# Modulation blocks 8 to 19 move from the head groups to the input projection, and small matmuls of the head groups alternate array halves

## The chip, the cores and the metric

The kernel runs on one core of a Trainium2 chip. The metric is the device time of one execution in microseconds (us), as the median of the runs. [...]

## The reference

One layer of a hybrid decoder, for a prompt of 512 tokens and for eight sample tokens. D is 2048, there are 16 attention and 16 RWKV-7 heads of 64.

```python
mod = jnp.dot(jax.nn.silu(c), P['ada_w'][l]) + P['ada_b'][l]     # (9, 2048) x (2048, 12288)
sh1, sc1, gt1, sh2, sc2, gt2 = jnp.split(mod, 6, axis=-1)
h = modulate(rmsnorm(x, P['norm1_g'][l]), sh1, sc1)
qa, ka, va, rkv0 = jnp.split(h @ w_in, [D_ATT, 2 * D_ATT, 3 * D_ATT], axis=-1)
...                                                              # attention heads -> att
wkv, y = wkv_scan(...)                                           # RWKV-7 heads -> rw
mix = jnp.concatenate([att, rw], axis=-1) @ P['w_out'][l]
x = x + gt1[:, None, :] * mix
h2 = modulate(rmsnorm(x, P['norm2_g'][l]), sh2, sc2)
gate, up = jnp.split(h2 @ P['w_gu'][l], 2, axis=-1)
x = x + gt2[:, None, :] * ((jax.nn.silu(gate) * up) @ P['w_down'][l])
```

The modulation has nine conditioning rows (one prompt, eight samples). Its 12288 columns are worked in 24 blocks of 512: blocks 0 to 7 are sh1 and sc1, which the input projection needs; 8 to 11 are gt1, 12 to 15 sh2, 16 to 19 sc2 and 20 to 23 gt2, which are first needed after the head groups.

## The kernel before

The program is one list of instructions for five engines. A scheduler sets each engine's order when the kernel is built, from its own timeline, so an engine takes its instructions strictly in that order on the chip, DMA issues included: nearly all loads and stores are issued by SP, in one queue.

It has these stages. **Start** (0 to about 200 us): normalise, transpose, modulation blocks 0 to 7. **LoRA** sums. **Input projection** (lines 783 to 802): 24 products, first the twelve of the RWKV columns (names p00 to p32), then the twelve of the attention columns (q00 to q32). Each product (line 133) covers 256 output columns by a Strassen scheme with seven PSUM banks, over eight pairs of k tiles, 21 matmuls a pair; weight columns come through two buffers (`raw`, two pairs each), are combined by VectorE (L143 to L146), split into a high and a low part by ScalarE and VectorE (L149, L150), and the seven sums are combined on VectorE (L163 to L170, tile c_p or c_q). After each pair of k tiles product calls `hook`, here `side` (line 783), which takes one step of the urgent generators (what follows on the last product: `rwkv_in`, `attn_in`) and, at every second call, one step of the lazy ones (`rwkv_pre`, bias table). All this side work shares one PSUM bank, the tag `ps`.

**Head groups** (lines 805 to 1297): for each of eight head pairs `rwkv_pair` (r), `chain` (c) and `attn_pair` (a), in the order of the string `SEQ_` at line 1282; `f3` there takes three steps of `todo`. `todo` holds modulation blocks 8 to 23 (line 865): `ada_steps` (line 231) loads four k tiles of 512 columns at a time (1 MB, tile raw_ada, two buffers), multiplies each k tile on its own column group of 32 (c_st holds the nine rows padded to 32), adds over k in PSUM (tile ada), copies the sum to SBUF and sums the four column groups by four matmuls with `sel4`. `rwkv_pair` makes, per pair: pg (the Gram products), a 16x16 inverse on VectorE that goes through DRAM both ways, then pq, px, pxt (64x64 each), pq and px of 32x32, pat, pgv, pu and pxa; `chain` walks the eight chunks (pch) and makes zy and z2; `attn_pair` makes pz (scores), pzt (transposes) and po (values), and the sample tokens' attention over the cache (K, V).

Where a loop runs over c or h outside and over the blocks i or b inside, all matmuls on one half of the array's rows (or columns) stand before those on the other half:

```python
for c in range(2):
    for i in range(8):
        mm(px[hb[c], i, :], Q[hb[c], i, :], XX[0][hb[c], i, :])
        mm(pxt[hb[c], i, :], XX[0][hb[c], i, :], Q[hb[c], i, :])
```

`hb` are the partitions 0 to 63 and 64 to 127. The output projection and the feed-forward part follow (from about 1505 us on).

## Time and profile before

| | us |
|---|---|
| median of three runs | 3356.26 (3343.64 to 3372.01) |
| the profiled execution | 3378.55 |
| its span, first to last instruction | 3376.8 |
| its mean granted clock | 0.918 |

| engine | busy us | share of the span |
|---|---|---|
| PE (matmul) | 2981.6 | 88% |
| DVE (VectorE) | 2480.9 | 73% |
| ACT (ScalarE) | 1278.0 | 38% |
| POOL (GpSimd) | 212.9 | 6% |

Busy time is the union of an engine's instructions; PEld is TensorE's weight load, which overlaps PE. Matmuls are pipelined, so a matmul's duration is longer than its distance to the next one. A group of rows gives the line of the kernel that issued it; line 90 is the helper `mm`, which all matmuls share, so groups are told apart by their tiles. An arrow in a row names what ended an engine's wait. The DMA share is the mean busy share of the core's 16 DMA engines.

### The profile page before, as it was taken

The page shows a single profiled execution, that of the slowest core. Times are in us where ns is not written, and L with a number is a line of the kernel's source. Part 1 is how long each engine was busy: PE and PEld are TensorE (multiplying, and loading weights), DVE is VectorE, ACT ScalarE, POOL GpSimd, SP SyncE. Part 2 cuts the span into 40 slices and gives each one's busy share as a digit, 9 for nine tenths or more (in the row PEclk, how much of TensorE's full clock was granted, in tenths as well). Part 3 has the DMA queues.
Part 4 walks back from the last instruction along what each step waited for, and adds up shares of the span by engine and source line. Part 5 has one row for each costly group of instructions (what it writes and reads, how often), then busy time and mean ns, then how long its engine had stood idle before and what let it go on. Part 6 is the DMA issues. An engine that isn't in the chain of part 4 may idle for free.

```text
span 3376.8 us, 59004 instructions
## 1 busy us (share of the span) xinstructions
PE 2981.6 (88%) x23282; PEld 2629.4 (78%) x23282; DVE 2480.9 (73%) x4846; ACT 1278.0 (38%) x2041; POOL 212.9 (6%) x216
## 2 busy tenths in 40 slices
PE   6987888999889999977977999999999987888988
PEld 2477787889746666656967999999999987787878
DVE  5666788777557455656878787778777788889786
ACT  3353343334223343444434333333333343334333
POOL 0100122110012111101000000000000000000000
PEclk8978999999858798887988999999999998999999
DMA  7744444444579798933322333333333332323223
GB/s 255 232 139 154 147 159 157 133 146 140 175 223 282 201 239 232 249 103 117 109 78 69 113 104 104 108 112 107 113 101 113 109 125 96 99 94 119 85 94 104
DMA packets 449194, 476.17 MB, mean 141 GB/s; under 512 B 84110, under 2 KB 360547, under 8 KB 448916
## 3 DMA queue, kind: packets, MB, share of 16 engines
q1 hardware_dynamic: 438736, 452.16, 43.4%
q10 hardware_dynamic: 7428, 11.65, 1.0%
q0 software_dynamic: 2752, 8.60, 0.8%
q8 instruction: 182, 2.98, 0.4%
q14 instruction: 96, 0.79, 0.1%
HBM read 409.10 MB, written 68.17 MB: 141 GB/s over the span
## 4 chain that ended last, share of the span: by engine, by line
PE 35%; DVE 28%; DMA 23%; issue 5%; ACT 5%; SPq 1%; POOL 1%; ACTq 0%; DVEq 0%; POOLq 0%
PE ada L90 4%; DMA raw_ada<-in_ada_w 2%; SPq L130 1%; PE po L90 1%; DVE x_a L125 1%; PE lx L90 1%; PE pg L90 1%; PE pz L90 1%; PE px L90 1%; DMA K<-in_cache_k 1%; PE pch L90 1%; PE pq L90 1%; DMA xb<-in_ada_w 1%; PE q22M L90 1%; PE q31M L90 1%
## 5 line engine op out<-in xcount | busy, mean ns | idle before, releaser
L90 PE MATMUL ada<-raw_ada,c_st 128*32 128x512 f32 x584 | 123.7, 763 | 17.5 <-DMA raw_ada<-in_ada_w 16.8
L90 PE MATMUL ada<-xb,c_st 128*32 128x512 f32 x184 | 69.9, 673 | 15.9 <-DMA xb<-in_ada_w 13.8
L1037 ACT ACTIVATE Sall<-pch,ppl 64x64 f32<-64x64 f32 x128 | 39.5, 309 | 75.5 <-PE pch L90 57.7
L1238 POOL TENSOR_TENSOR K<-K,qb 128x1024 f32<-128x1024 f32 (+2 forms) x24 | 58.2, 2440 | 147.5 <-DMA K<-in_cache_k 91.6
L1188 ACT ACTIVATE z<-z,mx 128x128 f32<-128x128 f32 (+3 forms) x64 | 35.8, 560 | 78.2 <-DVE mx L1187 37.9
L90 PEld LDWEIGHTS pg<-AR,BK 64*128 64x128 f32 x256 | 41.0, 237 | 22.7 <-issue 11.9
L90 PE MATMUL pz<-ak,aq 64*128 64x256 f32 (+3 forms) x128 | 55.3, 581 | 0.7 <-DMA ak<-pqd 0.7
L90 PE MATMUL pg<-AR,BK 64*128 64x128 f32 x256 | 49.1, 342 | 6.1 <-DMA AR<-abd 2.7
L90 PE MATMUL g0M<-x_g,g0hl 128*128 128x260 f32 x168 | 31.3, 348 | 21.7 <-ACT x_g L124 7.4
L90 PE MATMUL po<-zt,av 128*64 128x128 f32 x320 | 49.1, 310 | 0.4 <-ACT zt L1200 0.4
L90 PE MATMUL o0M<-x_m,o0hl 128*128 128x260 f32 x168 | 33.5, 366 | 17.6 <-ACT x_m L124 14.2
L901 DVE TENSOR_TENSOR GM<-pg,cst 128x512 f32<-128x512 f32 x32 | 22.0, 688 | 36.5 <-PE pg L90 36.3
L198 PEld LDWEIGHTS pzt<-ident,z 128*128 128x128 f32 x160 | 19.0, 155 | 37.5 <-ACT z L1190 13.0
L1184 DVE SCALAR_TENSOR_TENSOR z<-pz,rnq,T 128x128 f32<-128x128 f32 (+3 forms) x64 | 34.4, 546 | 18.3 <-PE pz L90 16.2
L90 PEld LDWEIGHTS g0M<-x_g,g0hl 128*128 128x128 f32 x168 | 27.5, 241 | 25.4 <-ACT x_g L124 8.7
L90 PEld LDWEIGHTS o0M<-x_m,o0hl 128*128 128x128 f32 x168 | 29.7, 259 | 21.6 <-ACT x_m L124 17.5
L1412 DVE SCALAR_TENSOR_TENSOR y<-c_d,modT,y 128x512 f32<-128x512 f32 x64 | 45.9, 751 | 0.0
L90 PEld LDWEIGHTS ada<-raw_ada,c_st 128*32 128x32 f32 x584 | 16.4, 119 | 37.4 <-DMA raw_ada<-in_ada_w 22.7
L1200 ACT COPY zt<-pzt 128x128 f32<-128x128 f32 (+3 forms) x64 | 26.5, 426 | 49.5 <-PE pzt L198 41.1
L90 PEld LDWEIGHTS po<-zt,av 128*64 128x64 f32 x320 | 34.2, 151 | 13.3 <-issue 6.8
L198 PE MATMUL pzt<-ident,z 128*128 128x128 f32 x160 | 33.8, 321 | 11.8 <-ACT z L1190 10.0
L1190 ACT ACTIVATE z<-z,mx 128x128 f32<-128x128 f32 (+3 forms) x64 | 35.5, 559 | 16.8 <-DVE mx L1189 11.6
(2104 smaller groups left out, 9215.3 us busy)
## 6 DMA issues: line engine op xcount, KB each, us to landing
raw_ada<-in_ada_w SPq DMA_DIRECT2D x64, 1024.0 KB
xb<-in_ada_w SPq DMA_DIRECT2D x92, 256.0 KB
actd<-c_u SPq DMA_DIRECT2D x22, 520.0 KB
a<-actd SPq DMA_DIRECT2D x22, 520.0 KB
raw_ada<-in_ada_w SPq DMA_DIRECT2D x36, 256.0 KB
lsd<-lx SPq DMA_DIRECT2D x12, 520.0 KB
prd<-rkv SPq DMA_DIRECT2D x24, 256.0 KB
K<-in_cache_k SPq DMA_DIRECT2D x16, 384.0 KB
```

The source lines that it names most:

```text
L90: pe.matmul(out, lhsT=lhsT, rhs=rhs, start=start, stop=stop)
L125: ve.tensor_sub(x[:, 1, o:e], src, x[:, 0, o:e].bitcast(F32))
L130: sp.dma_start(raw.rearrange("p (k m) c -> p k (m c)", k=2), src[k * P : (k + 2) * P, :].rearrange("(k p) m -> p k m", p=P))
L198: pe.transpose(out, in_=in_, identity=ident[:n, 0:n])
L901: ve.tensor_tensor(GM[i][:, :, :, h], pg, gmask.unsqueeze(2).to_broadcast([P, 2, 2, P]), op=ALU.mult)
L1037: ac.activation(S[hb[h], ch + 1, hb[h]], pc_[hb[h], ch, :], AF.Copy, scale=ppl[hb[h], pr, ch : ch + 1])
L1184: ve.scalar_tensor_tensor(z, in0=pz[:, :nk], scalar=rn[:, qi, h : h + 1], in1=Ts[h][:, 384 - 128 * qi :], op0=ALU.mult, op1=ALU.add)
L1188: ac.activation(z, z, AF.Exp, bias=mx[:, 0:1], accum_out=mx[:, 1:2])
L1190: ac.activation(z, z, AF.Copy, scale=mx[:, 2:3])
L1200: ac.copy(zt, pzt[:, :nk])
L1238: OK.tensor_mul(K[:n], K[:n], qb[:n])
L1412: ve.scalar_tensor_tensor(y[:, f, :SEQ], in0=c[:, j, :SEQ], scalar=modT[:, 48 + f, 0:1], in1=y[:, f, :SEQ], op0=ALU.mult, op1=ALU.add)
```

## The change

Twelve blocks of the modulation, 8 to 19, leave `todo` (`ADA` is 20 instead of 8) and become generators of the input projection, `ada_in`. A block is worked in two halves of 256 columns. A step of it loads four k tiles (512 KB, tile adr, one buffer), and the next step multiplies them on four column groups into the bank `ps`; the sum over the four steps is made in SBUF (tile adm) by one ScalarE copy and three VectorE adds. Two matmuls with `sel4` and one VectorE add end a half block. `side` takes a step of `adas` at every call that is not one of the lazy ones. The tile `sel` of the LoRA stage moves to the pool of that stage, and `tp`'s tag m1 goes.

In the head groups, loops are turned so that neighbouring matmuls use different halves: pg (the second head in a bank of psa instead of pa), pq, px, pxt, the 32x32 pq and px, pat, pgv, pu, pxa (both c at once, in two banks), z2, pz and po. What each computes stays the same.

The diff, without the turned loops of the 32x32 products and of pu:

```diff
--- before.py
+++ after.py
@@ -470,7 +470,7 @@
         OT, OR, OX = ve, ve, ve
         DQ, DB, DN = sp, ac, sp
         NW2 = 2
-        NBIG, ADA, ADB, SD, SE, SF = 4, 8, 24, 2, 4, 2
+        NBIG, ADA, ADB, SD, SE, SF = 4, 20, 24, 2, 4, 2
 
         with tc.tile_pool(reuse_waits="tile", name="lora", bufs=1) as lp:
             def lt(name, n=TOK):
@@ -519,7 +519,7 @@
                 ac.copy(wv[:, :, 0], wm)
                 ve.tensor_sub(wv[:, :, 1], wm, wv[:, :, 0].bitcast(F32))
                 w4s += [w4[:, k] for k in range(8)]
-            sel = tp.tile([P, HS], F32, tag="m1", name="sel", bufs=1)[:, :192].rearrange("p (m i e) -> p m i e", m=2, i=3)
+            sel = lp.tile([P, 192], F32, name="sel").rearrange("p (m i e) -> p m i e", m=2, i=3)
             iv = ident.rearrange("p (g m e) -> p m e g", g=2, m=2)
             for i in range(3):
                 ve.tensor_reduce(sel[:, :, i], iv, axis=AX.X, op=ALU.add)
@@ -778,16 +778,40 @@
                     DQ.dma_start(tabd[:, i * 320 : (i + 1) * 320], tab)
                 DQ.dma_start(skew, bass.AP(tensor=tabd.tensor, offset=tabd.offset, ap=[[640, NH], [0, P], [1, 640]]))
 
-            urgent, lazy, idle, count = [], [], [], [0]
+            def ada_in(blk):
+
+                for hf in range(2):
+                    c0, b2 = blk * 512 + hf * 256, slice(blk * 4 + 2 * hf, blk * 4 + 2 * hf + 2)
+                    m = ip.tile([P, 256], F32, tag="adm", name=f"adm{blk}{hf}", bufs=1)
+                    for k in range(0, KT, 4):
+                        raw = ip.tile([P, 4, 256], F32, tag="adr", name=f"adr{blk}{hf}{k}", bufs=1)
+                        sp.dma_start(raw, ada_w[k * P : (k + 4) * P, c0 : c0 + 256].rearrange("(j p) c -> p j c", p=P))
+                        yield
+                        o = psf(f"ao{blk}{hf}{k}")
+                        for j in range(4):
+                            mm(o[32 * j : 32 * j + 32, :256], c_st[:, k + j, :], raw[:, j])
+                        if k == 0:
+                            ac.copy(m, o[:, :256])
+                        else:
+                            ve.tensor_add(m, m, o[:, :256])
+                    o = psf(f"as{blk}{hf}")
+                    for j in range(2):
+                        mm(o[:, 9 * j : 9 * j + 9], m[:, j * 128 : (j + 1) * 128], sel4[:, :9])
+                    ve.tensor_tensor(modT[:, b2.start - 32 : b2.stop - 32, :], o[:, :18].rearrange("p (j c) -> p j c", j=2),
+                                     adab[:, b2].unsqueeze(2).to_broadcast([P, 2, 9]), op=ALU.add)
+
+            urgent, lazy, adas, count = [], [], [], [0]
 
             def side():
                 count[0] += 1
                 step(urgent)
                 if count[0] % SD == 0:
-                    step(lazy or idle)
+                    step(lazy)
+                else:
+                    step(adas)
 
             lazy.append(bias_table())
-            idle += [ada_side(b) for b in range(8, ADA)]
+            adas += [ada_in(b) for b in range(8, ADA)]
             for rk in range(2):
                 for q in range(4):
                     for j in range(3):
@@ -797,7 +821,7 @@
                         urgent.append((rwkv_in, attn_in)[rk](q, j, c))
                 if rk == 0:
                     lazy.append(sample_in())
-            while urgent or lazy or idle:
+            while urgent or lazy or adas:
                 side()
         pha.close()
 
@@ -891,14 +915,14 @@
 
                 GM = [dg(f"GM{pr}{i}").rearrange("p (c b h t) -> p c b h t", b=2, c=2, h=2) for i in range(2)]
                 for i in range(2):
+                    pg = [f(f"pg{pr}{i}{h}").rearrange("p (b c t) -> p c b t", b=2, c=2) for h, f in enumerate((pa, psa))]
+                    for b in range(2):
+                        for c in range(2):
+                            cc = slice((4 * i + 2 * b + c) * 128, (4 * i + 2 * b + c + 1) * 128)
+                            for h in range(2):
+                                mm(pg[h][:, c, b, :], BK[hb[h], cc], AR[hb[h], cc])
                     for h in range(2):
-                        rows = slice(h * 64, h * 64 + 64)
-                        pg = pa(f"pg{pr}{i}{h}").rearrange("p (b c t) -> p c b t", b=2, c=2)
-                        for b in range(2):
-                            for c in range(2):
-                                cc = slice((4 * i + 2 * b + c) * 128, (4 * i + 2 * b + c + 1) * 128)
-                                mm(pg[:, c, b, :], BK[rows, cc], AR[rows, cc])
-                        ve.tensor_tensor(GM[i][:, :, :, h], pg, gmask.unsqueeze(2).to_broadcast([P, 2, 2, P]), op=ALU.mult)
+                        ve.tensor_tensor(GM[i][:, :, :, h], pg[h], gmask.unsqueeze(2).to_broadcast([P, 2, 2, P]), op=ALU.mult)
 
                 def gm(b, c, h, rows, cols):
                     return GM[b // 2][rows, c, b % 2, h, cols]
@@ -949,33 +973,36 @@
                                          m1[hb[c]].unsqueeze(1).unsqueeze(1).to_broadcast([64, 2, 2, E]), op=ALU.mult)
                 E1f = E1.rearrange("p b h t -> p (b h) t")
                 pq = psa(f"pq{pr}").rearrange("p (i t) -> p i t", t=E)
-                for c in range(2):
-                    for i in range(8):
+                for i in range(8):
+                    for c in range(2):
                         mm(pq[hb[c], i, :], E1f[hb[c], i, :], XX[1][hb[c], i, :])
                 Q = tb(f"Q{pr}", 512).rearrange("p (i t) -> p i t", t=E)
                 ac.copy(Q, pq)
                 px = psa(f"px{pr}").rearrange("p (i t) -> p i t", t=E)
                 pxt = psa(f"pxt{pr}").rearrange("p (i t) -> p i t", t=E)
-                for c in range(2):
-                    for i in range(8):
+                for i in range(8):
+                    for c in range(2):
                         mm(px[hb[c], i, :], Q[hb[c], i, :], XX[0][hb[c], i, :])
+                for i in range(8):
+                    for c in range(2):
                         mm(pxt[hb[c], i, :], XX[0][hb[c], i, :], Q[hb[c], i, :])
...
@@ -988,36 +1015,38 @@
 
                 AG = wi.tile([P, 8, 2, E], F32, tag="ag", name=f"AG{pr}", bufs=NAG)
                 pat = psa(f"pat{pr}")
-                for c in range(2):
-                    for b in range(4):
+                for b in range(4):
+                    for c in range(2):
                         mm(pat[hb[c], b * 128 : (b + 1) * 128], ARv[:, b, 3 * c, :], ident)
                 ac.copy(AG[:, :, 1, :], pat.rearrange("p (i e) -> p i e", e=E))
                 pgv = psa(f"pgv{pr}")
-                for c in range(2):
-                    for i in range(8):
+                for i in range(8):
+                    for c in range(2):
                         mm(pgv[hb[c], i * 64 : i * 64 + 64], gm(i // 2, c, i % 2, hb[1 - c], hb[c]), UV[hb[1 - c], i // 2 * 2 + c, i % 2, :])
                 ac.copy(AG[:, :, 0, :], pgv.rearrange("p (i e) -> p i e", e=E))
...
                 Mt = wl.tile([P, 4, 2, E], F32, tag="mt", name=f"Mt{pr}", bufs=NMT)
+                pxa = [psa(f"pxa{pr}{c}") for c in range(2)]
+                for i in range(8):
+                    o_ = i // 2 * 64
+                    for c in range(2):
+                        mm(pxa[c][hb[i % 2], o_ : o_ + 64], AG[hb[c], i, 1, :], X2[hb[c], i, :])
+                for i in range(8):
+                    b, h = i // 2, i % 2
+                    o_ = 256 + b * 64
+                    for c in range(2):
+                        mm(pxa[c][hb[h], o_ : o_ + 64], XA[hb[c], b, h, :], BKt[hb[c], 2 * b + c, h * 64 : h * 64 + 64])
                 for c in range(2):
-                    pxa = psa(f"pxa{pr}{c}")
-                    for i in range(8):
-                        o_ = i // 2 * 64
-                        mm(pxa[hb[i % 2], o_ : o_ + 64], AG[hb[c], i, 1, :], X2[hb[c], i, :])
-                    for i in range(8):
-                        b, h = i // 2, i % 2
-                        o_ = 256 + b * 64
-                        mm(pxa[hb[h], o_ : o_ + 64], XA[hb[c], b, h, :], BKt[hb[c], 2 * b + c, h * 64 : h * 64 + 64])
-                    ac.copy(ARv[:, :, 3 * c, :], pxa[:, :256].rearrange("p (b t) -> p b t", b=4))
-                    ve.tensor_tensor(Mt[:, :, c, :], pxa[:, 256:].rearrange("p (b t) -> p b t", b=4),
+                    ac.copy(ARv[:, :, 3 * c, :], pxa[c][:, :256].rearrange("p (b t) -> p b t", b=4))
+                    ve.tensor_tensor(Mt[:, :, c, :], pxa[c][:, 256:].rearrange("p (b t) -> p b t", b=4),
                                      eye2.unsqueeze(1).to_broadcast([P, 4, E]), op=ALU.add)
                 return lambda: chain(pr, AR, Mt, UV, BKt, GM, gm, bv)
 
@@ -1055,10 +1084,10 @@
                         n0 = 1 if q == 0 and c == 0 else 0
                         ac.copy(Y[hb[1 - c], 2 * q + n0 : 2 * q + 2], zy[hb[1 - c], c + 2 * n0 :: 2, :])
                     z2 = psz(f"z2{pr}{q}").rearrange("p (b e) -> p b e", b=4)
-                    for c in range(4):
+                    for n in range(8):
+                        c, h = n // 4 * 2 + n % 2, n // 2 % 2
                         b, R_ = 2 * q + c // 2, hb[1 - c % 2]
-                        for h in range(2):
-                            mm(z2[R_, c // 2, h * 64 : h * 64 + 64], gm(b, c % 2, h, slice(0, 128), R_), UV[:, 4 * q + c, h, :])
+                        mm(z2[R_, c // 2, h * 64 : h * 64 + 64], gm(b, c % 2, h, slice(0, 128), R_), UV[:, 4 * q + c, h, :])
                     ve.tensor_add(Y[:, q2], Y[:, q2], z2[:, :2])
                 if LT == 2 and late:
                     late.pop()()
@@ -1176,12 +1205,12 @@
 
                 def scores(qi):
                     nk = 128 * (qi + 1)
+                    pzs = [pst(f"pz{pr}{h}{qi}") for h in range(2)]
                     for h in range(2):
-                        hr = slice(h * 64, h * 64 + 64)
-                        pz = pst(f"pz{pr}{h}{qi}")
-                        mm(pz[:, :nk], q[hr, qi * 128 : (qi + 1) * 128], kn[hr, :nk])
+                        mm(pzs[h][:, :nk], q[hb[h], qi * 128 : (qi + 1) * 128], kn[hb[h], :nk])
+                    for h in range(2):
                         z = tz(f"z{pr}{h}{qi}", nk)
-                        ve.scalar_tensor_tensor(z, in0=pz[:, :nk], scalar=rn[:, qi, h : h + 1], in1=Ts[h][:, 384 - 128 * qi :],
+                        ve.scalar_tensor_tensor(z, in0=pzs[h][:, :nk], scalar=rn[:, qi, h : h + 1], in1=Ts[h][:, 384 - 128 * qi :],
                                                 op0=ALU.mult, op1=ALU.add)
                         mx = sm("mx", [P, 3], 4)
                         ve.tensor_reduce(mx[:, 0:1], z, axis=AX.X, op=ALU.max, negate=True)
@@ -1200,10 +1229,9 @@
                         ac.copy(zt, pzt[:, :nk])
                         zts[qi, h] = zt
                     po = pst(f"po{pr}{qi}")
-                    for h in range(2):
-                        hr = slice(h * 64, h * 64 + 64)
-                        for j in range(qi + 1):
-                            mm(po[hr, :128], vt_[:, j, hr], zts[qi, h][:, j * 128 : (j + 1) * 128], start=(j == 0), stop=(j == qi))
+                    for j in range(qi + 1):
+                        for h in range(2):
+                            mm(po[hb[h], :128], vt_[:, j, hb[h]], zts[qi, h][:, j * 128 : (j + 1) * 128], start=(j == 0), stop=(j == qi))
                     ve.tensor_copy(at[:, qi * 128 : (qi + 1) * 128], po[:, :128])
 
                 scores(0)
```

## Rows read from the trace of the kernel before

**Rows 1.** Stretches: us, busy (xN) PE, PEld, DVE, ACT, POOL; PEclk, DMA share, GB/s

```profile
239.00:578.00 339.00, 287.86 (x2137) 271.91 (x2136) 250.69 (x488) 125.11 (x183) 50.09 (x61) 0.96 0.48 155
578.00:897.00 319.00, 302.06 (x2342) 294.41 (x2342) 245.12 (x524) 123.20 (x160) 31.29 (x36) 0.96 0.41 132
897.00:1505.00 608.00, 552.70 (x5241) 374.58 (x5241) 337.75 (x822) 226.99 (x611) 95.77 (x76) 0.80 0.81 226
```

**Rows 2.** Chain of waits by line, share of 897:1505, then of 239:578

```profile
by line: PE ada L90 11.4%; DMA raw_ada<-in_ada_w 7.5%; PE po L90 5.3%; PE pg L90 4.7%; PE pz L90 4.7%; PE px L90 4.7%; DMA K<-in_cache_k 4.6%; PE pch L90 4.1%; PE pq L90 4.0%; issue 3.6%; PE pzt L198 3.0%; PE pxt L90 3.0%; PE zy L90 2.3%; D
by line: issue 7.9%; PE p00M L90 6.4%; DMA p01w<-in_w_in 5.7%; DMA p12w<-in_w_in 3.9%; DMA p11w<-in_w_in 3.9%; DMA p32w<-in_w_in 3.7%; DMA p31w<-in_w_in 3.1%; DMA p02w<-in_w_in 3.0%; PE p02M L90 2.9%; DMA p21w<-in_w_in 2.7%; DMA pld<-lsd 2.
```

**Rows 3.** PE groups, 897:1505: tiles, shapes, xcount, busy us, mean ns, idle us

```profile
L90 PE MATMUL ada<-raw_ada,c_st 128*32 128x512 f32 x512 | 92.8, 773 | 15.2 <-DMA raw_ada<-in_ada_w 15.2
L90 PE MATMUL ada<-sel,adac 128*128 128x9 f32 x128 | 19.2, 277 | 0.1
L90 PE MATMUL pg<-AR,BK 64*128 64x128 f32 x256 | 49.1, 342 | 6.1 <-DMA AR<-abd 2.7 <-DVE GM L901 2.1 <-DVE rb L857 0.8
L90 PE MATMUL po<-zt,av 128*64 128x128 f32 x320 | 49.1, 310 | 0.4 <-ACT zt L1200 0.4
L90 PE MATMUL px<-XX,Q 64*64 64x64 f32 x256 | 40.5, 267 | 0.1
L90 PE MATMUL pq<-XX,E 64*64 64x64 f32 x256 | 22.0, 265 | 0.0
```

**Rows 4.** PE in order of time: start, us, engine, line, op, tiles, shapes, xcount

```profile
137.58 0.88 PE L90 MATMUL l_2M<-x_h,l_2hl 128*128 128x264 f32 x5
138.39 1.04 PE L90 MATMUL ada<-xb,c_st 128*32 128x512 f32 x2
...
1248.01 0.70 PE L90 MATMUL pz<-ak,aq 64*128 64x256 f32 x2
...
1256.16 1.07 PE L90 MATMUL ada<-raw_ada,c_st 128*32 128x512 f32 x8
1257.16 0.37 PE L90 MATMUL px<-X,Q 32*32 32x32 f32 x6
...
1452.73 0.70 PE L90 MATMUL pz<-ak,aq 64*128 64x256 f32 x4
...
1468.93 1.58 PE L90 MATMUL pat<-ident,AR 128*64 128x128 f32 x16 [0.93 <-DVE X L979]
1470.44 1.90 PE L90 MATMUL pgv<-UV,GM 64*64 64x64 f32 x32
...
1480.51 0.63 PE L90 MATMUL pxa<-BKt,XA 64*64 64x64 f32 x16
```

**Rows 5.** Weight loads of the modulation in 897:1505: ns min/median/max, first, last start

```profile
L236 SPq DMA_DIRECT2D raw_ada<-in_ada_w x64: 368/390/3451, 915.0 to 1449.8; - x64
```

**Rows 6.** Stretches inside the head groups, columns as in rows 1

```profile
897.00:976.00 79.00, 54.30 (x232) 32.30 (x232) 32.26 (x89) 15.07 (x40) 10.08 (x9) 0.57 0.92 266
976.10:1013.60 37.50, 37.50 (x255) 22.79 (x255) 24.55 (x49) 9.81 (x28) 2.04 (x2) 0.50 0.62 195
1221.80:1279.80 58.00, 55.47 (x587) 37.81 (x585) 35.98 (x96) 27.83 (x76) 5.58 (x5) 1.00 0.95 256
1450.50:1494.90 44.40, 40.01 (x498) 29.49 (x498) 25.10 (x64) 25.22 (x68) 7.34 (x5) 1.00 0.45 127
```

**Rows 7.** Thirty ns of pch alone: busy (xN) PE, PEld, ACT, as rows 1

```profile
1482.20:1482.23 0.03, 0.02 (x2) 0.02 (x2) 0.00 (x0) 1.00 0.94 256
```

**Rows 8.** A product (columns as rows 3) and one VectorE addition from PSUM

```profile
L90 PE MATMUL q30M<-x_h,q30hl 128*128 128x264 f32 x168 | 22.2, 288 | 0.0
L165 DVE TENSOR_TENSOR c_p<-c_p,p00M x1: 422/422/422, 263.9 to 263.9; 128x264 f32<-128x264 f32 x1
```

**Rows 9.** SP waits, 897:1505: us in total, times, longest

```profile
SPq L236 <- PE ada L90: 87.2, 28, 10.3
```

## What the change does to the time

> **What bounds the kernel now.** I read the stretches first. They split the span at two edges that the diff touches: the input projection in two halves (RWKV columns 239 to 578 us, attention columns 578 to 897), then the head groups (897 to 1505) [rows 1]. The rest of the kernel, the start and all after 1505, is left as it is. In the head groups TensorE is busy 552.7 of 608.0 us, VectorE 337.8, ScalarE 227.0, and the DMA engines 0.81 of the time; the granted clock is 0.80. So TensorE bounds this stage, with the DMA engines next. The chain agrees: its largest parts there are the modulation's matmuls, 11.4%, and the landing of their weights, 7.5% [rows 2]. In the first half of the input projection it is different: TensorE is busy 287.9 of 339.0 us, so 51 us are free, and the chain runs through the landing of weight columns (p01w 5.7%, p12w and p11w 3.9% each) more than through matmuls [rows 2]. In the second half only 17 us are free [rows 1]: there TensorE is the bound.
>
> Then I read what TensorE's time in the head groups is made of [rows 3], and the order of single groups of matmuls in time [rows 4], to see which small matmuls already run side by side.
>
> **What leaves the head groups.** Each f32 matmul of the code is two records. Blocks 8 to 23 cost 92.8 us for 512 records of 128x512 and 19.2 us for 128 of the 9-column sums [rows 3]. Twelve of sixteen blocks go: 0.75 x 112.0 = 84 us. A group's busy time contains the tail of its last matmul, which the next group overlaps: one visit of eight records is 1.07 us long, but the next begins 1.00 us after it [rows 4]. So I count 0.94 x 84 = 79 us. Their weights go too: 48 of the 64 loads [rows 5], each 4 x 128 x 512 x 4 bytes, 50.3 MB; at this stage's mean, 226 GB/s at a share of 0.81, they take 50.3 MB / 279 GB/s = 180 of its 492 us of DMA time. What is left on the queue is the start: the first fill still waits for its weights, now those of block 20.
>
> **What the alternation brings.** The new order puts matmuls on the two row halves or column halves of the array next to each other. Does the chip run them side by side? Where the old code already does so, yes: sixteen records of pxa (64 columns streamed, halves alternate) take 0.63 us, 39 ns each, while 32 of pgv (same size, eight matmuls on one half before the other) take 1.90 us, 59 ns each, both in a stretch at full clock [rows 4, 6]. Row halves do it as well: four records of pz with 256 columns, both heads together, take 0.70 us, and two, one head by itself, take 0.70 us as well [rows 4], again both at full clock. I therefore take half of what is serial now: pg 49.1, po 49.1, px with pxt (they take turns, so 40.5 is one time for both), pq 22.0 [rows 3], and once a pair, eight times, pgv with 1.90 and pat with 1.58 [rows 4]: (49.1 + 49.1 + 40.5 + 22.0 + 15.2 + 12.6) / 2 = 94 us. The 32x32 products, pu, pz, pxa and z2 are short, or in part side by side already; I give them 34 us together, an estimate from their shares. That is 128, less the tails as above 120 us. TensorE's work would fall by 79 + 120 = 199 to 354 us, about VectorE's 338.
>
> [...]
>
> **How much of it the stage gives back.** Not all of 199: VectorE, DMA landings and the round trips of the inverse come next. [...] From the other side, 60% of the 199 is 119. I take -115. Two banks get tighter: pg's second head takes one of the two psa banks, and pxa holds both until ScalarE and VectorE have read them, so the next product of the pair waits where one bank stood free before; that is a few waits a pair, and part of the lower bound. Bounds: -60 if VectorE and the round trips hold the pace near today's, -170 if 85% comes back.
>
> **What the input projection pays.** 96 visits (12 blocks, 2 halves, 4 groups of four k tiles), one at every second of the 192 hooks. Each is four matmuls of 128x32 with 256 columns on four column groups. Four of 512 columns take 1.00 us [rows 4]; half the columns is not below 0.50 and not above 1.00; I take 0.57, since the fixed part is small beside the streaming. Going in and out costs too: in the start, five product records between two such visits take 0.81 us, where a product on its own runs 168 records in 22.2 us, 0.132 each, so 0.15 more [rows 4, 8]. Together 0.72 x 96 = 69 us. The nine-column sums: 24 half blocks at half of 19.2/16 = 0.6 us, 14 us. In all 83 us of TensorE, 41.5 per half. In the second half this lies on the bound: +41. In the first, 51 us are free; the chain there runs through weights and VectorE, so TensorE can take some in its gaps: I count a third of the gaps as filled, +25. VectorE gets 72 adds of at most 0.42 us [rows 8] and 24 of 0.2, some 35 us on 496 of 658; ScalarE 24 copies. They fit into the idle fourth, but each lies ahead of weight work in VectorE's order. The SP queue gets 96 loads of 512 KB, moved past weight columns, bounces and stores; 50.3 MB raise its DMA share from 0.45 to about 0.61. With one buffer, each load waits on SP until the previous visit's matmuls are done, and the next weight columns wait behind it; the weights have two buffers ahead. I add 11 us: +77. Bounds +45 (gaps filled, no queueing) and +155 (below). The PSUM bank of the side work is now shared with 120 more uses; that sits in the same 11.
>
> The moved selector tile costs nothing: the same three reductions, in another pool.
>
> **Sum.** The profiled execution took 3378.55 us (span 3376.8). -115 + 77 = -38: 3340.5 us on its terms. It lay 22 us over the median of the runs, 3356.26; on the median's terms 3318 us.
>
> **Rivals.**
> 1. The head groups give nearly all back: -170, and the first half of the projection hides more, +60: -110, 3246 us. For it: VectorE and DMA would be at 0.55 to 0.7 there. Against: one order fixed for all engines, and waits that TensorE's work hid.
> 2. Slower, by the SP queue. In the head groups SP stood for the modulation's matmuls 28 times, 87.2 us, 3.1 us each [rows 9], with two buffers. With one, at 96 visits, if half of that reaches the products through late weight columns, a visit costs 1.6 us instead of 0.8: +154, net +39, 3395 us. It decides from 1.2 us a visit on (115 / 96). For it: the chain of the first half already runs through weight landings. Against: the two weight buffers reach some 14 us ahead (each holds a quarter of a product's 339 / 12 = 28 us).
> 3. The head groups follow little (-70), as VectorE, round trips and K and V loads take over: net +7, 3363 us. For it: K landings are 4.6% of the chain there [rows 2]. [...]
> [...]
>
> **How the numbers follow.** Forecast 0.50, rival one 0.17, two 0.15, three 0.13, four 0.05. A measurement of this kernel can tell about 1%, 33.6 us, from no change. The forecast's own range is 3281 to 3346 (head groups and projection each off by about 25); two thirds of it, 0.33, is faster by over 1%. Faster 0.33 + 0.17 = 0.50; within 1%: 0.17 + 0.13 + 0.05 = 0.35; slower 0.15. The range from 3245 to 3392 leaves out rival two's upper part and what lies beyond rival one.
>
> **What would show it.** Right: the head groups some 490 us long with TensorE near 350 busy; px and po with half the busy time; about 80 us more before them, TensorE above 0.95 in both halves; SP waits for the new loads short. Wrong: weight landings (p..w) growing on the chain of the first half, SP standing long on the new load; the granted clock of the head groups falling toward 0.5, which would take the halving back; or busy times of px and pq unchanged.

## The result, and the profile after

The changed kernel took 3546.82 us as the median of four runs (3537.55 to 3549.69), the kernel before, run beside it, 3364.14. The ratio is 1.0546, with an interval from 1.0499 to 1.0593: 5.5% slower, 183 us. The forecast was 3318 us and a range up to 3392, so it failed in sign and in range.

The profiled execution after has a span of 3547.1 us, 170.3 longer than before. The edges, each the first or last matmul of its kind in the trace, show where: the last product of the input projection ends at 1038 us (895 before, +143), the head groups take 654.5 us from the first pg to the first matmul of the output projection (632.1 before, +22), and between the two lie 4 us more. What follows is equally long, 1843.7 and 1843.0 us.

Stretches of the kernel after: us, then busy time and count of PE, PEld, DVE, ACT, POOL, granted clock (a share of full speed), DMA share, GB/s; they answer [rows 1].

```profile
239.00:582.00 343.00, 306.40 (x2428) 276.22 (x2429) 246.66 (x491) 121.73 (x177) 34.73 (x44) 0.96 0.60 193
582.00:1038.00 456.00, 379.26 (x2756) 331.25 (x2754) 273.68 (x573) 135.16 (x187) 36.99 (x54) 0.83 0.49 159
1038.00:1673.00 635.00, 463.96 (x4920) 319.99 (x4921) 337.30 (x855) 223.07 (x608) 88.77 (x76) 0.73 0.53 148
```

The first half of the projection is hardly longer (343 for 339). The second grew from 319 to 456 while TensorE's work grew only from 302 to 379: its idle time went from 17 to 77 us. In the head groups TensorE's work fell by 89 us (552.7 to 464.0), yet the stretch is 27 us longer and the idle time grew from 55 to 171. So neither stage is bound by TensorE as it was. In the head groups the granted clock is also lower (0.73, before 0.80).

PE groups of the kernel after in 1038:1673, columns as in [rows 3]: tiles, shapes, count, busy us, mean ns, idle time before them.

```profile
L90 PE MATMUL pg<-AR,BK 64*128 64x128 f32 x256 | 42.6, 331 | 11.0 <-DMA BK<-abd 6.8 <-DVE Mt L1049 2.3 <-DVE adm L796 1.0
...
L90 PE MATMUL po<-zt,av 128*64 128x128 f32 x320 | 41.4, 317 | 11.3 <-DVE z L1213 9.3 <-DVE at L1235 1.1 <-ACT zt L1229 0.7
...
L90 PE MATMUL ada<-raw_ada,c_st 128*32 128x512 f32 x128 | 22.2, 746 | 11.3 <-DMA raw_ada<-in_ada_w 11.3
...
L90 PE MATMUL pq<-XX,E 64*64 64x64 f32 x256 | 18.8, 313 | 16.1 <-DMA XX<-xd 15.8
...
L90 PE MATMUL px<-XX,Q 64*64 64x64 f32 x256 | 12.8, 270 | 1.5 <-ACT Q L980 1.5
...
L90 PE MATMUL ao<-adr,c_st 128*32 128x256 f32 x96 | 10.8, 531 | 24.4 <-DMA adr<-in_ada_w 19.9 <-DVE smq L721 3.7 <-ACT tok L743 0.7
```

px fell from 40.5 to 12.8 us, but that isn't all gain: before, px and pxt took turns, so 40.5 us was one time for both. Together they were busy 43.8 us before and 22.7 after, so alternation about halved them. The last row doesn't belong here: 96 of the 768 records of the projection's visits, twelve visits, run in the head groups, up to 1126 us.

**A gap in the second half.** PE in order of time, kernel after, between the last matmul of q11 (764 us) and the first of q12 (start, length, tiles, count, and in brackets the idle time before it and what ended it):

```profile
764.18 0.64 PE L90 MATMUL ao<-adr,c_st 128*32 128x256 f32 x8 [0.19 <-DVE pv L691]
...
767.69 0.87 PE L90 MATMUL pss<-bd,t 128*128 128x2 f32 x4 [2.86 <-DVE adm L796]
771.84 1.08 PE L90 MATMUL ao<-adr,c_st 128*32 128x256 f32 x8 [3.29 <-DMA adr<-in_ada_w]
773.46 1.02 PE L90 MATMUL as<-sel,adm 128*128 128x9 f32 x4 [0.53 <-DVE adm L796]
774.75 3.93 PE L90 MATMUL pn<-bd,asq 128*128 128x2 f32 x20 [0.27 <-DVE modT L800]
779.00 0.59 PE L198 MATMUL pn<-ident,c_q 128*8 128x128 f32 x2 [0.33 <-DVE ast L710]
781.95 0.66 PE L198 MATMUL psb<-ident,t 128*128 128x128 f32 x2 [2.37 <-DVE smq L721]
783.27 1.12 PE L198 MATMUL pt<-ident,c_q 128*128 128x128 f32 x4 [0.65 <-DVE t L676]
785.17 1.08 PE L90 MATMUL ao<-adr,c_st 128*32 128x256 f32 x8 [0.78 <-DVE tok L741]
786.75 1.11 PE L198 MATMUL pk<-ident,tok 128*128 128x128 f32 x4 [0.49 <-ACT adm L794]
...
793.18 2.13 PE L90 MATMUL q12M<-x_h,q12hl 128*128 128x264 f32 x8 [1.79 <-ACT c_q L163]
```

For 29 us no product runs. ao, as, pss, psb, pn, pt, pk and pbs (in the part left out) all use the one PSUM bank `ps` and take turns in it: each waits until VectorE or ScalarE has read the turn before, one ao also for its weights. q12 at last waits for c_q of q11 (L163): its seven banks are free only once the combination has read them, and that needs a tile of `pair_tile`, three of which exist, each held until the side work of an older product is through. Counted in order, the pn, pt and pk of this gap are those of q01, three products before q11. In the second half of the kernel after the gaps between products add up to 135 us, nearly all of the 143; seven of them last 10 to 29 us. Before, they add up to 2.

**The pairs.** PE in order of time around the end of pxa of a pair in the kernel after:

```profile
1286.46 0.68 PE L90 MATMUL pxa<-BKt,XA 64*64 64x64 f32 x23
...
1289.40 1.50 PE L90 MATMUL pg<-AR,BK 64*128 64x128 f32 x8 [2.26 <-DVE Mt L1049]
```

pg of the fifth pair waits for Mt of the third, VectorE's reading of pxa's bank. So pg runs in step with pxa: in the kernel after, the last pg of a pair starts within 6 us of the first pxa of the pair before, in all seven cases (pg 1108, 1219, 1285, 1378, 1442, 1527, 1609 us, pxa 1108, 1214, 1285, 1378, 1442, 1524, 1603). Before, it was 31 to 97 us ahead (pg 928, 1039, 1090, pxa 1026, 1074, 1143, and so on). The VectorE line that reads pg, in the kernel before and then after (ns min/median/max, first and last start):

```profile
L901 DVE TENSOR_TENSOR GM<-pg,cst x32: 672/692/692, 903.8 to 1367.6; 128x512 f32<-128x512 f32 x32
```

```profile
L925 DVE TENSOR_TENSOR GM<-pg,cst x32: 672/692/692, 1051.0 to 1608.9; 128x512 f32<-128x512 f32 x32
```

A pair's inverse starts from GM. After pg come the inverse, through DRAM and VectorE, and then pq to pxa, and these now stand one pair behind the other: pq of the eight pairs starts from 1076 to 1632 us, a pair in 79 us, before from 976 to 1441, a pair in 66. The last GM, at 1608.9 (1367.6 before), leaves 65 us to the last z, the last pair's chain with nothing beside it.

### The profile page after: what moved, and what is told of

It reads as the page before. It is cut to its first block, busy times and chain, and to the rows that moved or that the text cites. A ratio compares the mean times of both kernels' runs of the same rounds, so it can differ in the third digit from the quotient of the medians.

```text
span 3547.1 us, 60020 instructions
## 1 busy us (share of the span) xinstructions
PE 2995.9 (84%) x23666; PEld 2620.5 (74%) x23666; DVE 2503.6 (71%) x4930; ACT 1279.7 (36%) x2053; POOL 195.6 (6%) x216
## 4 chain that ended last, share of the span: by engine, by line
DVE 19%; PE 14%; DMA 12%; ACT 3%; issue 3%; SPq 1%; ACTq 0%; DVEq 0%; POOLq 0%
SPq L130 1%; DMA a<-actd 1%; DVE x_a L125 1%; PE u0M L90 1%; PE u10M L90 0%; PE u1M L90 0%; PE u17M L90 0%; PE g17M L90 0%; PE g1M L90 0%; PE g19M L90 0%; PE u15M L90 0%; PE u9M L90 0%; PE d23M L90 0%; DVE x_g L125 0%; PE d03M L90 0%
## 5 line engine op out<-in xcount | busy, mean ns | idle before, releaser
L90 PE MATMUL ao<-adr,c_st 128*32 128x256 f32 x768 | 71.7, 446 | 68.4 <-DMA adr<-in_ada_w 58.3
L90 PEld LDWEIGHTS ao<-adr,c_st 128*32 128x32 f32 x768 | 16.8, 115 | 86.7 <-issue 44.9
L90 PE MATMUL ada<-raw_ada,c_st 128*32 128x512 f32 x200 | 51.5, 709 | 12.7 <-DMA raw_ada<-in_ada_w 11.9
L796 DVE TENSOR_TENSOR adm<-adm,ao 128x256 f32<-128x256 f32 x72 | 29.9, 415 | 43.5 <-PE ao L90 43.4
L1267 DVE TENSOR_REDUCE lg<-K 128x16 f32<-128x1024 f32 (+2 forms) x24 | 29.1, 1213 | 35.7 <-POOL K L1266 35.6
L1217 ACT ACTIVATE z<-z,mx 128x128 f32<-128x128 f32 (+3 forms) x64 | 35.8, 559 | 50.3 <-DVE mx L1216 49.4
L90 PE MATMUL pg<-AR,BK 64*128 64x128 f32 x256 | 42.6, 331 | 11.0 <-DMA BK<-abd 6.8
L90 PE MATMUL po<-zt,av 128*64 128x128 f32 x320 | 41.4, 317 | 11.3 <-DVE z L1213 9.3
L1079 DVE TENSOR_TENSOR UV<-UV,zy 64x256 f32<-64x256 f32 (+1 forms) x32 | 12.3, 383 | 45.6 <-PE zy L90 45.3
L90 PEld LDWEIGHTS po<-zt,av 128*64 128x64 f32 x320 | 25.2, 154 | 24.6 <-DVE z L1213 9.8
```

What stands on the lines that cost most here:

```text
L90: pe.matmul(out, lhsT=lhsT, rhs=rhs, start=start, stop=stop)
L796: ve.tensor_add(m, m, o[:, :256])
L1079: ve.tensor_add(u, u, zy[hb[c], c + n0 :: 2, :])
L1217: ac.activation(z, z, AF.Exp, bias=mx[:, 0:1], accum_out=mx[:, 1:2])
L1267: ve.tensor_reduce(lg[:n, i, :], K[:n].rearrange("p (g e) -> p g e", e=E), axis=AX.X, op=ALU.add)
```

## The experiments

A visit is one load and use of four k tiles of 256 columns. The edges in us of every kernel, from its own trace:

| kernel | first half ends | second half ends | first pg | first o0 | pg to o0 |
|---|---|---|---|---|---|
| before | 576 | 895 | 902 | 1534 | 632 |
| after | 583 | 1038 | 1049 | 1703 | 655 |
| e1_alt_only | 574 | 890 | 897 | 1618 | 722 |
| e2_move_only | 587 | 1040 | 1051 | 1674 | 623 |
| e3_pg_old | 580 | 1031 | 1043 | 1644 | 601 |
| e4_alt_pg_old | 575 | 896 | 903 | 1509 | 606 |
| e5_few_loads | 573 | 990 | 999 | 1658 | 660 |
| e7_p_half | 583 | 928 | 934 | 1523 | 589 |
| e8_gp_queue | 584 | 1051 | 1058 | 1724 | 665 |
| e9_loads_only | 596 | 928 | 936 | 1467 | 532 |
| e10_none_alt | 573 | 894 | 902 | 1428 | 526 |
| e11_none_old | 574 | 894 | 900 | 1461 | 561 |
| e12_half_loads | 574 | 894 | 901 | 1465 | 564 |
| e13_small_products | 577 | 1001 | 1008 | 1608 | 601 |
| e14_few_loads_pg_old | 575 | 996 | 1006 | 1565 | 559 |

Single runs of the kernel before lay between 3343.6 and 3400.7 us over these groups, their median between 3356.6 and 3378.0, so the edges of the traces carry the smaller differences. They are single traces too: the projection of before, e1, e4, e10, e11 and e12, which is the same in all six, ends between 890 and 896 us, and what follows o0, the same code in all fifteen kernels, takes 1842 us (e11) to 1871 us (e7).

### The two halves of the change, and pg

```diff
 e1_alt_only, e4_alt_pg_old (on the kernel after)
-NBIG, ADA, ADB, SD, SE, SF = 4, 20, 24, 2, 4, 2
+NBIG, ADA, ADB, SD, SE, SF = 4, 8, 24, 2, 4, 2
 e3_pg_old, e4_alt_pg_old (on the kernel after)
-pg = [f(...) for h, f in enumerate((pa, psa))] 
+for h in range(2): pg = pa(...)                
 e2_move_only: all of the head groups' lines as before
```

> The changed kernel with ADA = 8: all sixteen blocks stay in the head groups, nothing is added to the input projection; the head loops are turned as in the change. Theory P (the second head of pg stands in a psa bank, so a pair's Gram products wait for the pxa of the pair before): the input projection ends near 897 us as before, but the head groups keep a period of about 75 us a pair, 610 to 650 us long, so the time is 3360 to 3410 us. Rival Q (the head groups of the changed kernel were held up only by the twelve visits that spilled into them and by what came late from the projection): they shrink to 500 to 550 us, and the time is 3260 to 3310 us. Forecast on record for the alternation alone: about 60% of 120 us, 3285 us.

> Only the modulation's move (ADA = 20, ada_in, side, sel); the head groups' loops as in the kernel before. Theory L (the projection's side work goes one visit after the other: one buffer adr, one bank ps, an order fixed for all; a visit takes 9 us and not two hooks' 7): the projection's end moves from 897 to about 1038 us, the head groups give back 50 to 80 us, so 3356 + 141 - 65 = 3400 to 3450 us. Rival (the forecast on record: projection +77, head groups -50 to -79): 3355 to 3385 us. Rival S (the turned loops changed the order the scheduler gave to the projection too): projection end below 980 us.

> The changed kernel with one loop put back: pg as before, its two heads one after the other in the bank pa. Theory P: pg runs ahead again, the period of a pair falls below 67 us, the head groups from 624 to 500 to 550 us, so the time falls from 3547 to 3425 to 3480 us. Rival Q (spill and lateness from the projection): nothing moves by more than 10 us, 3535 to 3555 us. If the granted clock of the head groups (0.73) is what holds them: within 20 us of the changed kernel.

> No move (ADA = 8), pg as before, all other loops turned as in the change. Theory P: head groups 520 to 570 us instead of 608, so 3285 to 3330 us, and 50 to 100 us below the run with the alternation whole. Rival Q: the same as that run within 15 us. If the turned loops bring nothing at all since VectorE and round trips set the pace: 3345 to 3370 us.

Alternation alone: 3483.68 us, ratio 1.0364 (1.0298 to 1.0429). With pg as before: 3355.82, ratio 0.9975 (0.9936 to 1.0014). So pg in psa by itself costs 116 us of head groups (722 to 606) and 128 us of time, more than the 50 to 100 of theory P, and rival Q falls: nothing is moved here, and the serial pairs are there all the same. VectorE's GM in e1 and then in e4, columns as above:

```profile
L925 DVE TENSOR_TENSOR GM<-pg,cst x32: 674/692/693, 898.7 to 1519.5; 128x512 f32<-128x512 f32 x32
```

```profile
L925 DVE TENSOR_TENSOR GM<-pg,cst x32: 669/692/693, 904.8 to 1357.6; 128x512 f32<-128x512 f32 x32
```

With pg in `pa` the last GM is 162 us earlier. But e4 itself isn't the 3285 to 3330 us of theory P: without a move the other turned loops brought no gain in the time, as its third expectation said, though 26 us in the head groups. In the changed kernel the same step costs less: e3 took 3498.84 us, ratio 1.0417 (1.0355 to 1.0478), head groups 655 to 601. That is a gain, as P said, but 50 to 100 us short of the length it expected, and the time is outside its 3425 to 3480 us: something else holds them there.

The move alone: 3512.54 us, ratio 1.0443 (1.0367 to 1.0520). The projection ends at 1040, as theory L said, and the turned loops have no part in it; but the head groups give back 9 us where 50 to 80 were expected.

### What makes the projection long

```diff
 e5_few_loads (on after) and e14 (on e3):
-    raw = ip.tile(..."adr"...); sp.dma_start(raw, ...)
+    if k == 0: raw = ip.tile(..."adr"...); sp.dma_start(raw, ...)
 e8_gp_queue (on after):
-    sp.dma_start(raw, ...)
+    gp.dma_start(raw, ...)
 e9_loads_only (on e3): no o, no matmuls; ac.copy / ve.tensor_add read raw[:, k // 4]
 e13_small_products (on e3):
-    mm(o[32 * j : 32 * j + 32, :256], c_st[:, k + j, :], raw[:, j])
+    mm(o[32 * j : 32 * j + 32, :8], c_st[:, k + j, :], raw[:, j, :8])
     at k == 0: ac.copy(m, raw[:, 0]); at every k: ve.tensor_add(m[:, :8], m[:, :8], o[:, :8])
```

> The changed kernel, but of the four loads of a half block only the first is issued; the later three visits multiply the same four k tiles again (so blocks 8 to 19 of the modulation get wrong values). 24 loads instead of 96; all 96 visits with their matmuls, copies and adds stay. Theory L1 (a visit is slow because with one buffer its load can only start when the visit before has read it, and lands 6 to 8 us later): the projection's end falls from 1038 us to below 970 and no visit is left behind it; the time falls by 100 us or more, to 3400 to 3450 us. Theory L2 (a visit is slow because all side work takes turns in one PSUM bank in an order fixed at the build, load or no load): the projection's end stays above 1000 us, the time above 3500 us.

> The changed kernel with the 96 loads of adr issued by GpSimd's queue instead of SP's. Rival SP (weight columns wait behind a load that stands on SP for its buffer): the projection's end falls from 1038 to below 960 us, the time to 3430 to 3470 us. Theories L1 and L2: within 25 us of the changed kernel, 3520 to 3570 us, since the loop of one buffer and the order of the bank are the same.

> The changed kernel with pg as before, and the 96 visits without their matmuls and without the bank ps: a visit loads its 512 KB and one VectorE add (or ScalarE copy) of 256 columns reads it; the values of blocks 8 to 19 are not computed. Theory L2 (turns in the bank ps, and TensorE's work): the second half of the projection ends at 900 to 935 us instead of 1031, and nothing is left over for the head groups. Rival: the loads themselves (DMA share, the SP queue) are what delays the products: it ends above 970 us.

> The changed kernel with pg as before; all 96 loads and all turns in the bank ps stay, but a visit's four matmuls stream 8 columns instead of 256, and its add reads 8 columns (blocks 8 to 19 are then not the modulation's). So TensorE's work for the visits nearly goes, some 60 of 83 us, and the number of turns in the bank stays. If TensorE's work delays the products: the projection ends near the 928 us of the run with loads alone, below 950. If the turns do (an order fixed over one bank, each turn a wait on VectorE or ScalarE): above 980 us, and visits still spill.

Loads that stand on SP aren't it: with GpSimd's queue the kernel took 3594.37 us, 48 more than after, outside both expectations. There the loads stand in an engine with other work, and the queue shows what they wait for (us in total, times, longest):

```profile
POOL adr L788 <- PE ao L90: 538.3, 81, 23.7
```

It is the visit before, 6.6 us at a time: with one buffer the loop goes load, landing, turn in the bank. (Theory L1 had put the landing at 6 to 8 us. In the kernel after, where TensorE waited for it, a visit's first matmul began 4.8 us after the issue as a median of 23.) But the loads are the smaller part: with a quarter of them the second half still ended at 990 (3524.7 us), between the ends that L1 and L2 expected, and twelve visits were still left over; its time is that of L2. And loads without turns cost little (3327.09 us in all, the second half ending at 928, as L2 said). Stretches of e9, columns as above:

```profile
240.00:596.00 356.00, 296.50 (x2135) 281.23 (x2133) 266.38 (x543) 129.43 (x196) 54.29 (x65) 0.92 0.73 233
596.00:928.00 332.00, 306.88 (x2341) 296.06 (x2340) 250.22 (x562) 127.93 (x170) 23.39 (x34) 0.95 0.59 186
```

With 50.3 MB more the DMA share of the halves is 0.73 and 0.59, and they are 33 us longer together (20 and 13). When the visits keep their loads and turns but stream 8 columns instead of 256, the second half ends at 1001 (3469.55 us), so the turns hold it more than TensorE's work does. On e3's terms the projection's 136 us are 33 for the loads and the adds that read them, 73 for the turns with hardly any matmul time in them, and 30 for the 256 columns. The 73 aren't the bank's alone: in e13 a turn still comes behind its load, and TensorE stood 13.7 us of the second half for landings (ao <- DMA adr in its waits). These are steps of one order of removal; since all of it shares one loop, another order would divide it otherwise (e14 puts the loads at 35).

How far the side work is behind can be counted in the traces. By the hooks 48 visits belong to each half. In the changed kernel 36 stand before the first matmul of q00, twelve fewer; behind the last product, twelve are left; so too in e2, e3, e5, e8 and e14 (37 and twelve in e13). In the trace of the kernel after, VectorE's 4930 instructions and SP's 1626 DMA issues start in the order of the build, line for line. I take these counts to be that order's as well, whatever a visit costs on the chip: e5 has a quarter of the loads and the same counts, 36 and twelve. Twelve visits are 24 hooks, three products: as many as there are tiles of `pair_tile`. I read it so: the order lets the side work slip by three products in the first half, which costs next to nothing there (+7 us); after that each product stands behind side work and waits as long as that takes. Its pace in the second half is 456 / 12 = 38 us a product, against 27 before.

```diff
 e7_p_half (on e3):
-NBIG, ADA, ADB, SD, SE, SF = 4, 20, 24, 2, 4, 2
+NBIG, ADA, ADB, SD, SE, SF = 4, 12, 24, 2, 4, 2
```

> Four blocks (8 to 11) go to the input projection instead of twelve, 32 visits, all of which fit into its first half, where 36 visits of the changed kernel moved the end by 6 us; pg as before, the other head loops turned. No visit spills into the head groups, the second half of the projection is as before. If the cost of the move sits in the second half and in the spill: projection end at 900 to 912 us, the head groups 20 to 40 us shorter than the 583 of the run with pg as before and no move (28 us of TensorE work and a quarter of the weights are gone), 3300 to 3345 us. If the visits cost alike wherever they stand (1.5 us of path each): 3355 + 47 - 30 = 3370 us.

e7 was my attempt at a version that gains: it took 3384.39 us, ratio 1.0017 (0.9985 to 1.0050), no gain. No visit stands in its second half, yet that is 26 us longer (345 against 319). Of the 16 half pairs of rwkv_pre ten were through with their last turn (pbs) by the end of the first half before, seven in e7: the debt of the first half is paid in the second. Its head groups take 589 us, and its trace reaches o0 at 1523 us, eleven before the kernel before; but it is also the trace with the longest rest (1871 us against 1843), so how much of the missing gain is the change's stays open.

### What the head groups give back

```diff
 e10_none_alt (on e3), e11_none_old (on e2):
-adas += [ada_in(b) for b in range(8, ADA)]
+gp.memset(modT[:, :48, :], 0.0)
 e12_half_loads (on e4), in ada_steps: a load only at k0 % 8 == 0
```

> The changed kernel with pg as before and blocks 8 to 19 left out altogether (their values are zero): no visit, no load of theirs anywhere; the other head loops turned. It shows what the head groups give back when nothing spills into them. From the first pg matmul to the first matmul of the output projection the kernel before takes 632 us, the one with pg as before and no move 606. Forecast on record: 632 - 115 = 517 us, TensorE near 350 busy. Rival V (VectorE, the round trips through DRAM and the order set the pace): 560 to 600 us. Time 3355 less the same difference.

> Blocks 8 to 19 left out altogether as in the run beside it, but all loops of the head groups as before. Forecast: the 79 us of TensorE stay about 60% to 100% on the path, 632 - 50 to 632 - 79, 553 to 582 us from the first pg to the output projection, and the turned loops of the run beside it win another 40 to 70. Rival V: within 15 us of the run beside it.

> No move (ADA = 8), pg as before, the other head loops turned, and in the head groups only every second load of the modulation's weights is issued (each is multiplied twice, so these values are wrong); TensorE's work is the same, 33.6 MB of loads are gone. If the DMA engines (share 0.85 there, 0.95 in the first 116 us) took over when TensorE's matmuls got shorter: 606 falls to 560 to 585 us. If VectorE and round trips hold the pace: 597 to 610 us.

> The changed kernel with pg as before and, as in the run with few loads, only the first load of each half block (the later three visits multiply the same tiles again; these values are wrong). There two visits were left behind the projection's end, and eleven in the changed kernel. If the left visits are what keeps the head groups long (601 us with pg as before, against 526 with nothing left): 540 to 560 us from the first pg to the output projection, and 3400 to 3430 us in all. If the late side work of the attention columns itself keeps them long (pn, pt and pk of the last products, which also wait for the bank): 575 us or more, 3440 us or more.

Stretches of the head groups of e10, then of e11, columns as above:

```profile
897.00:1428.00 531.00, 424.75 (x4806) 293.07 (x4805) 335.90 (x845) 223.75 (x613) 95.16 (x78) 0.80 0.62 167
```

```profile
895.00:1461.00 566.00, 503.04 (x4810) 368.88 (x4810) 333.71 (x845) 224.04 (x614) 93.81 (x78) 0.76 0.59 157
```

With nothing left over, the head groups answer as forecast: 632 to 561 without the twelve blocks (-71, expected 50 to 79), and to 526 with the loops turned as well (-106, forecast -115). The whole kernels took 3310.15 and 3287.47 us, 64 and 86 less than the kernel before beside them (3373.74), so not all that the head groups gave reached the total of these few runs. Rival V falls: VectorE's 336 us fit into 531. TensorE's busy time went down by 78 us through alternation here (503.0 to 424.8), not by 120, and the stage by 35, a little under the 40 to 70 of e11's expectation.

Between e10's 526 and e3's 601 stand 75 us. The move's loads aren't it: e9 has them and takes 532. What e3 has besides is the projection's leftovers. In e14 (3421.24 us, as the first expectation said, though not for its reason: twelve visits are left in e5 and e14 too, not two) the last visit is done at 1067, 71 us after the last product, and the head groups take 559; in e3 at 1125, 95 us after, and they take 601; in e13 at 1085, 83 us after, and 601 again. pz, the first matmul of the attention, starts 23 us after pg in e10, 89 in e14, 110 in e3, 117 in e13. The visits carry with them the attention columns' own side work, which takes turns with them (the last pt ends at 908 before, 1133 in e3). Whether the visits or that work hold the head groups, these runs don't part: both go and come together. Nor do they part the leftovers from the granted clock. A stretch of e3's head groups, columns as above:

```profile
1031.00:1644.00 613.00, 496.37 (x4979) 336.80 (x4979) 357.70 (x897) 228.91 (x622) 93.39 (x78) 0.72 0.57 157
```

From the first pg to the first o0, TensorE is idle for 102 us in e10 and 107 in e3, but busy for 424 and 494. The leftovers' own matmuls are some 24 of these 70 us. The others are matmuls that both kernels have and that took longer in e3, at a granted clock of 0.72 against 0.80 (pz 56.5 and 62.1 us, po 40.6 and 45.6).

Why e4, without a move, gained only 26 us of head groups from 57 us less TensorE time (560.9 to 503.7 from the first pg to the first o0), e12 shows. Stretches of e4, then of e12, columns as above:

```profile
897.00:1013.00 116.00, 86.53 (x727) 50.67 (x727) 63.17 (x149) 32.73 (x89) 18.48 (x15) 0.72 0.95 280
897.00:1509.00 612.00, 505.70 (x5291) 317.65 (x5291) 349.67 (x863) 231.43 (x626) 97.19 (x78) 0.78 0.82 228
```

```profile
897.00:1465.00 568.00, 488.21 (x5286) 311.98 (x5286) 335.50 (x858) 229.98 (x624) 93.17 (x78) 0.83 0.67 185
```

With half of the modulation's loads the head groups fell from 606 to 564 (3312.98 us) with the same matmuls, as the first expectation said. So in e4 the loads of sixteen blocks hold the head groups when the matmuls get shorter. The granted clock was higher as well (0.83 against 0.78), and TensorE's time 17 us less, so the 42 us aren't the loads' alone.

No kernel with the whole computation was faster than the one before; the intervals of e4 and e7 hold 1. No run gives adr a second buffer, the visits a bank of their own, or pg's second head a bank outside psa.

## Why the prediction was wrong, step by step

**What leaves the head groups** (79 us of TensorE): the stage became 71 us shorter in e11. TensorE's busy time fell by only 50 (552.7 to 503.0), at a granted clock of 0.76 against 0.80, so the 71 isn't those 79 alone.

**What the alternation brings** (120 us): too large. 57 to 78 were measured without pg, which after went from 49.1 to 42.6 and not to half. The halving held for px with pxt (43.8 to 20.8 us together) and roughly for pq; not for po. One PE group of the kernel before in 897:1505, then those of e4 in 897:1509, columns as in [rows 3]:

```profile
L90 PE MATMUL pxt<-Q,XX 64*64 64x64 f32 x256 | 39.9, 264 | 0.0
```

```profile
L90 PE MATMUL po<-zt,av 128*64 128x128 f32 x320 | 43.1, 324 | 0.6 <-ACT zt L1229 0.6
...
L90 PE MATMUL pq<-XX,E 64*64 64x64 f32 x256 | 12.3, 231 | 0.0
L90 PE MATMUL px<-XX,Q 64*64 64x64 f32 x256 | 11.8, 227 | 2.1 <-ACT Q L980 2.1
...
L90 PE MATMUL pxt<-Q,XX 64*64 64x64 f32 x256 | 10.7, 231 | 0.0
```

po was priced by pxa of [rows 4], with 64 streamed columns; it streams 128 with all 128 rows, and gained 6 of the 24.5 us; that the shape is the reason isn't shown. The 34 us for the small rest were 14.

**How much the stage gives back** (-115): near in size (-106 in e10) where nothing else stands in the way, wrong in the kernel as changed. No run shows the 60% of the 199: in e10 the stage gave back 106 us for 128 us less of TensorE's busy time (552.7 to 424.8). +22 was measured, and by the runs it is 632 - 106 + 75 (e10 to e3: the leftovers and the lower clock that came with them) + 53 (pg in psa, e3 to after) = 654. Two terms failed.
- "pg's second head takes one of the two psa banks ... that is a few waits a pair, and part of the lower bound": this named the right bank and mis-sized it: 53 us in the kernel after, 116 in e1. I counted waits on TensorE. What I missed was an order: before, pg of the next pair was complete before pxa of this one because `pa` belonged to it alone. In psa it takes turns with this pair's products, so two pairs hardly overlap. So -60 was no bound.
- The leftovers weren't in the sum at all. I spread the 96 visits over the 192 hooks and took it for granted that they would be done in time.

**What the input projection pays** (+77, bounds 45 and 155): measured +143, inside the bounds and near the upper one. TensorE's cost was near: where a visit stood between products in the trace after (at 250, 258, 755 and 845 us), the next product began 0.56 to 0.57 us after it, as estimated, against 1.00 for 512 columns [rows 4]; ao is busy for 71.7 us over its 768 records (69 expected, with 55 of it for the matmuls themselves), as for 16.6 (14). The term that failed is the 11 us for loads, bank and queues: on e3's terms 33 for the loads and 73 for the turns. The DMA share of 0.61 was also a slip of the sum: 50.3 MB at 279 GB/s are 180 us, 0.27 of the 658, so 0.72 by the same rows; e9 shows 0.66 over both halves. "The PSUM bank of the side work is now shared with 120 more uses; that sits in the same 11" is the sentence. It asked for the length of a turn, not for what waits behind it: products, through three tiles. Also "In the first, 51 us are free" was right by itself (+7 there), but what the first half saved it passed on, as e7 shows.

**Rival two**, slower by the SP queue, had the sign and nearly the price (from 1.2 us a visit; 143 / 96 = 1.5), but not the place: the new loads' waits on SP were short, 1.4 us each for the visit before and 2.4 for its load, 121 us in all (rows of the kernel after, 239:1130, that answer [rows 9], us, times, longest), and another queue made it worse.

```profile
SPq L788 <- PE ao L90: 73.7, 54, 4.8
SPq L788 <- DMA adr<-in_ada_w: 47.7, 20, 4.4
```

**Rival four**, 0.05 of the chances: no run shows its term. px with pxt, and pq, were busy about half as long in e4 (43.8 to 20.8 us, 22.0 to 12.3). **What would show it**: "TensorE above 0.95 in both halves" was the right test; it came out at 0.89 and 0.83.

## What to carry to other kernels

Before work is added to a bank, buffer or tile that several generators share, ask what each user of it holds while it waits: here side turns of some 2 us each (twelve in the gap of 29 us) held a product's output tile, and three such tiles were all the slack there was. A tile that moves into a shared pool takes that pool's order too; look in the trace for what ran ahead only because it had a bank of its own. Work that fits a stage by its hooks can still stand late in the order, so count what is done at the stage's end.

## What the runs showed of the hardware

px and pxt each write the results of both array halves into one bank, in different partitions, and their busy time together (they took turns before) fell from 43.8 to 20.8 us in e4 when the halves alternate; pq, alone in its bank, fell from 22.0 to 12.3.

Less work on TensorE didn't raise the granted clock in a steady way. It is 0.80 in the head groups before (a mean: stretches of it were at 0.50, others at 1.00 [rows 6]), where TensorE is busy 91% of the time, 0.80 in e10 at 80%, 0.83 in e12 at 86%, but 0.73 after at 73% and 0.76 in e11 at 89%. Nor did shorter matmuls move it one way: with the loops turned it went from 0.76 (e11) to 0.80 (e10), and from 0.80 (before) to 0.78 (e4). How much of the loss after is the clock's was not separated.
